# Float32 decoder trunk on one core: weight halves made by GpSimd transfers (cast, then accumulate) in place of a raw buffer and a subtraction

## The chip, the cores and the metric

The kernel runs on one core of one Trainium2 chip. The metric is the device time of one execution in microseconds (us). Below, PE is the matrix engine, ACT the scalar engine, DVE the vector engine, POOL the GpSimd engine and SP the engine that mostly issues transfers. Each of SP, ACT and POOL can issue transfers in its own queue, and each engine works through its instructions strictly in the order in which they stand.

## The reference, cut to what matters

Two layers over 512 tokens of width 1024, everything in float32:

```
for l in range(DEPTH):
    h = rmsnorm(x, g_mix[l])
    dq, dk, dv, c_q, c_kv_kr, xq, gate_logits = split(h @ w_in[l])
    y_diff = diff_attention(dq, dk, dv, ...) @ w_diff_o[l]        # 8 heads, causal
    y_mla  = latent_attention(c_q, c_kv_kr, ...) @ w_mla_o[l]     # 8 heads, causal
    y_mem  = memory_cross_attention(xq, mem_n, ...) @ w_cross_o[l]
    gates  = sigmoid(gate_logits + b_gate[l])
    merged = gates[0] * y_diff + gates[1] * y_mla + gates[2] * y_mem
    x = x + merged @ w_out[l]
    x = x + square(relu(rmsnorm(x, g_mlp[l]) @ w_mlp1[l])) @ w_mlp2[l]
```

## The kernel before

**Three multiplications for one.** PE multiplies in a reduced float format (`fp32r` in the profile). To keep float32 accuracy each operand is split into a high part `hi`, which is the value rounded to that format, and a low part `lo = value - hi`. The helper `mm3` (L108 to L111) then issues three matmuls into the same sum: hi·hi (L109), one cross term (L110) and the other (L111).

**Weight units.** All weights are cut on the host into units of at most 128 x 1024 numbers (512 KB), 320 in all, listed in `units` in the order of use. A unit goes through three stages. `load_raw` (L901) has SP transfer it into one of `RB` = 3 raw buffers `wraw`. `do_split` (L908) calls `split_into` (L100): ACT copies `wraw` into `whi` with rounding (L101), and DVE writes `wlo = wraw - whi` (L102). Then PE reads both. There are `NB` = 4 buffers each of `whi` and `wlo`, so splits run up to four units ahead of use and raw loads three further. The other activations are split by the same helpers: `split_scaled` (L104) makes ACT write hi (L105) and DVE lo (L106), both with a gain per row.

**Order of the work.** `prog` is a list of entries, one for each piece of a stage, with the units that it reads. `merge` interleaves attention entries with matrix products by a fixed plan, so that PE has products to do while ACT and DVE work on softmaxes. In each layer come the projections (`ck_item`, `cq_item`, `kvb_item`, `qb_item`, `diff_chunk`, gates), attention, the output projections (`y8_item`, `out_item`), and last the MLP: 32 `u_item` and 32 `w2_item`, one unit and 24 matmuls of 512 columns each. A scheduler turns the program order into one fixed order for each engine; it works with estimates of time, and the order is then fixed for the chip.

**The start.** `begin` (L293) has SP load the eight tiles of x, with the first three raw loads between them (`if k in (0, 2, 5): load_raw()`), and `feed` splits each x tile on ACT and DVE. The first product is `ck_item`, with three units.

**POOL** builds constants at the start and computes the power -1/2 in `rsq` (L131, L132) for the norms, 91 instructions of 128 x 2 to 128 x 8 numbers. Their results `f`, `of`, `r` are read by DVE (L587, L666 and others), and PE then transposes what DVE wrote (L591, L669). It issues no transfer.

Of the kernel before, what the change touches and what calls it, by code (L numbers as in the profile page):

```python
# [9 lines left out]
F32 = mybir.dt.float32  # L10
F32R = mybir.dt.float32r
AF = mybir.ActivationFunctionType
ALU = mybir.AluOpType
AX = mybir.AxisListType

P = 128
# [43 lines left out]
def tile_trunk(ctx: ExitStack, tc: tile.TileContext, x_t, mem_t, mem_n, pos, ifr, gcol, grow, w_ck, w_cq, w_kvb, w_qb,  # L60
               w_mem, w_xq, w_d, w_g, w_oc, w_om, w_od, w_out, w_1, w_2, out):
    nc = tc.nc
    V, A, G, T = nc.vector, nc.scalar, nc.gpsimd, nc.tensor

    def pool(name, bufs, **kw):
        return ctx.enter_context(tc.tile_pool(name=name, bufs=bufs, **kw))

    RB, NB = 3, 4
    cst = pool("cst", 1)
    sm = pool("sm", 2)  # L70
    pw_raw, pw_hi, pw_lo = pool("wraw", RB), pool("whi", NB), pool("wlo", NB)
    pools = {n: pool(n, b) for n, b in (("H", 16), ("O", 16), ("X", 8), ("G", 1), ("B", 24), ("scr", 5), ("PT", 4))}
    p_p = pool("P", 3)
    PS = {n: pool("ps_" + n, b, space=bass.MemoryType.PSUM) for n, b in (("acc", 2), ("s", 3), ("tp", 2), ("o", 1))}
    dram = pool("dram", 1, space=bass.MemoryType.DRAM)
# [2 lines left out]
    def nm(s):  # L78
        cnt[0] += 1
        return f"{s}{cnt[0]}"  # L80

    def tl(which, dt=F32):
        return pools[which].tile([P, 512], dt, tag=which, name=nm(which))
# [16 lines left out]
    def split_into(hi, lo, src):  # L100
        A.activation(out=hi, in_=src, func=AF.Copy)  # L101
        V.tensor_tensor(out=lo, in0=src, in1=hi, op=ALU.subtract)  # L102
# [116 lines left out]
    def feed(l, k, xt, gbase, dst, sqs):  # L219
        hi, lo = tl(dst, F32R), tl(dst, F32R)  # L220
        split_scaled(hi, lo, xt, gc[:, l, gbase + k:gbase + k + 1])
        if k == 0:
            A.activation(out=sqs, in_=xt, func=AF.Square)
        else:
            s = tl("scr")
            A.activation(out=s, in_=xt, func=AF.Square)
            V.tensor_tensor(out=sqs, in0=sqs, in1=s, op=ALU.add)
        return hi, lo

    def new_sqs():  # L230
        return tl("scr")
# [47 lines left out]
    def layer(l):  # L279
# [13 lines left out]
        def begin():  # L293
            if l == 0:
                sqs = new_sqs()
                h = []
                xts = []
                for k in range(KT):
                    xt = tl("X")
                    nc.sync.dma_start(out=xt, in_=x_t[k * P:(k + 1) * P, :])  # L300
                    xts.append(xt)
                    if k in (0, 2, 5):
                        load_raw()
                for k, xt in enumerate(xts):
                    h.append(feed(0, k, xt, C_MIX, "H", sqs))
                st["h"], st["sqs"] = h, sqs
            s["h"] = st["h"]
# [550 lines left out]
        def dpair(p):  # L858
            return diff_chunk(p, 0) + diff_chunk(p, 1) + diff_chunk(p, 2)

        e = [Entry(lambda w: begin())]
        gx = [gate_item(1, ft, "X") for ft in range(KT)]
        ym = [y4_item(w_om, "om", 1, fp, True) for fp in range(4)]
# [31 lines left out]
        prog.extend(layer(l))  # L895

    units = [ap for e in prog for ap in e.units]
    raws, splits = [], []
    consumed = 0

    def load_raw():  # L901
        ap = units[len(raws)]
        a, b = ap.shape[1], ap.shape[2]
        t = pw_raw.tile([P, 1024], F32, tag="wraw", name=nm("wraw"))
        nc.sync.dma_start(out=t[:, :a * b].rearrange("p (a b) -> p a b", a=a), in_=ap)
        raws.append((t, a, b))

    def do_split():  # L908
        t, a, b = raws[len(splits)]
        hi = pw_hi.tile([P, 1024], F32R, tag="whi", name=nm("whi"))  # L910
        lo = pw_lo.tile([P, 1024], F32R, tag="wlo", name=nm("wlo"))
        split_into(hi[:, :a * b], lo[:, :a * b], t[:, :a * b])
        splits.append(tuple(z[:, :a * b].rearrange("p (a b) -> p a b", a=a) for z in (hi, lo)))

    for i, e in enumerate(prog):
        if i == 0:
            e.fn([])
            continue
        while len(splits) < min(len(units), consumed + NB):
            while len(raws) < min(len(units), len(splits) + RB):  # L920
                load_raw()
            do_split()
        while len(raws) < min(len(units), len(splits) + RB):
            load_raw()
        n = len(e.units)
        e.fn(splits[consumed:consumed + n])
        consumed += n

# [80 lines left out]
```

## Time and profile before

| | |
|---|---|
| median of 3 runs | 2035.04 us (2034.2 to 2037.99) |
| the profiled execution | 2039.67 us, its span 2037.6 us, mean granted PE clock 0.994 |
| PE busy | 2005.1 us, 98% |
| weight loads of PE (beside the matmuls) | 1715.9 us, 84% |
| DVE busy | 1162.2 us, 57% |
| ACT busy | 917.4 us, 45% |
| POOL busy | 146.0 us, 7%, 121 instructions |
| transfers | 181 MB, mean 89 GB/s |

The span runs from the first to the last instruction; the execution's own time holds a little more around it. Busy times are those of the engine's own instructions. A matmul's end is modelled, so successive matmuls overlap in the records. In the groups of instructions a row reads: line, engine, operation, output <- inputs, shapes, count, busy us, mean ns of one, then the idle time just before and what ended most of it.

### The profile page before, as it was taken

The page shows a single profiled execution, that of the slowest core. Times are in us where ns is not written, and L with a number is a line of the kernel's source. Part 1 is how long each engine was busy: PE and PEld are TensorE (multiplying, and loading weights), DVE is VectorE, ACT ScalarE, POOL GpSimd, SP SyncE. Part 2 cuts the span into 40 slices and gives each one's busy share as a digit, 9 for nine tenths or more (in the row PEclk, how much of TensorE's full clock was granted, in tenths as well). Part 3 has the DMA queues.
Part 4 walks back from the last instruction along what each step waited for, and adds up shares of the span by engine and source line. Part 5 has one row for each costly group of instructions (what it writes and reads, how often), then busy time and mean ns, then how long its engine had stood idle before and what let it go on. Part 6 is the DMA issues. An engine that isn't in the chain of part 4 may idle for free.

```text
span 2037.6 us, 27922 instructions
## 1 busy us (share of the span) xinstructions
PE 2005.1 (98%) x11008; PEld 1715.9 (84%) x11008; DVE 1162.2 (57%) x2170; ACT 917.4 (45%) x1727; POOL 146.0 (7%) x121
## 2 busy tenths in 40 slices
PE   8999999999999999999999999999999999999999
PEld 7779997888878888888888899979897788888887
DVE  7755765777656543434447567757686454434442
ACT  6666654444433432323346666634445334323321
POOL 0300110111200000000002001101020000000000
PEclk9989999999999999999999999999999999999999
DMA  5233122222214333333332321222222333333332
GB/s 170 73 110 102 69 63 73 63 73 73 63 53 154 93 96 101 93 99 98 117 104 67 125 80 63 72 74 63 73 63 63 101 116 93 102 96 94 102 94 73
DMA packets 54675, 181.06 MB, mean 89 GB/s; under 512 B 6416, under 2 KB 7440, under 8 KB 54544
## 3 DMA queue, kind: packets, MB, share of 16 engines
q1 hardware_dynamic: 51840, 175.66, 27.8%
q10 hardware_dynamic: 2704, 3.62, 0.6%
q8 instruction: 87, 1.43, 0.3%
q14 instruction: 44, 0.36, 0.1%
HBM read 175.06 MB, written 4.19 MB: 88 GB/s over the span
## 4 chain that ended last, share of the span: by engine, by line
PE 95%; ACT 2%; DVE 1%; DMA 1%; issue 0%; POOL 0%; ACTq 0%; DVEq 0%; POOLq 0%
PE psacc L109 21%; PE psacc L111 20%; PE psacc L110 20%; PE pss L109 7%; PE pss L111 7%; PE pss L110 7%; PE pss L610 2%; PE pss L613 2%; PE pso L642 2%; PE pstp L654 1%; PE pstp L638 1%; PE pstp L591 1%; PE pso L110 1%; PE pso L111 1%; PE pso L109 1%; PE pstp L479 1%
## 5 line engine op out<-in xcount | busy, mean ns | idle before, releaser
L101 ACT ACTIVATE whi<-wraw 128x1024 fp32r<-128x1024 f32 (+3 forms) x320 | 334.5, 1046 | 751.7 <-PE psacc L110 398.5
L102 DVE TENSOR_TENSOR wlo<-wraw,whi 128x1024 fp32r<-128x1024 f32 (+3 forms) x320 | 385.9, 1206 | 97.7 <-ACT whi L101 95.4
L109 PE MATMUL psacc<-H,whi 128*128 128x512 f32 x816 | 321.6, 394 | 2.6 <-ACT B L561 2.2
L110 PE MATMUL psacc<-H,whi 128*128 128x512 f32 x816 | 320.2, 392 | 0.0
L111 PE MATMUL psacc<-H,wlo 128*128 128x512 f32 x816 | 320.1, 392 | 0.0
L109 PE MATMUL psacc<-whi,H 128*128 128x256 f32 (+1 forms) x928 | 271.6, 294 | 10.3 <-ACT whi L101 6.8
L110 PE MATMUL psacc<-wlo,H 128*128 128x256 f32 (+1 forms) x928 | 265.1, 286 | 0.0
L111 PE MATMUL psacc<-whi,H 128*128 128x256 f32 (+1 forms) x928 | 264.3, 287 | 0.2 <-DVE H L106 0.2
L109 PE MATMUL pss<-O,whi 128*128 128x512 f32 x640 | 249.8, 392 | 1.6 <-ACT O L105 1.6
L110 PE MATMUL pss<-O,whi 128*128 128x512 f32 x640 | 250.8, 392 | 0.0
L111 PE MATMUL pss<-O,wlo 128*128 128x512 f32 x640 | 250.5, 392 | 0.0
L109 PEld LDWEIGHTS psacc<-whi,H 128*128 128x128 f32 x928 | 177.6, 192 | 17.8 <-ACT whi L101 6.8
L109 PEld LDWEIGHTS psacc<-H,whi 128*128 128x128 f32 x816 | 153.2, 188 | 36.0 <-ACT B L561 2.6
L111 PEld LDWEIGHTS psacc<-H,wlo 128*128 128x128 f32 x816 | 153.2, 188 | 33.6 <-issue 2.0
L110 PEld LDWEIGHTS psacc<-H,whi 128*128 128x128 f32 x816 | 153.3, 188 | 31.4 <-issue 0.7
L110 PEld LDWEIGHTS psacc<-wlo,H 128*128 128x128 f32 x928 | 178.2, 192 | 1.8 <-issue 1.0
L111 PEld LDWEIGHTS psacc<-whi,H 128*128 128x128 f32 x928 | 177.3, 192 | 1.0 <-DVE H L106 0.4
L840 DVE TENSOR_TENSOR X<-psacc,X 128x512 f32<-128x512 f32 x64 | 44.3, 692 | 207.1 <-PE psacc L111 207.1
L627 ACT ACTIVATE P<-pss,nmx 128x128 f32<-128x128 f32 (+2 forms) x224 | 115.1, 521 | 73.6 <-DVE nmx L624 47.5
L109 PEld LDWEIGHTS pss<-O,whi 128*128 128x128 f32 x640 | 120.4, 188 | 27.3 <-ACT O L105 2.0
L110 PEld LDWEIGHTS pss<-O,whi 128*128 128x128 f32 x640 | 121.1, 189 | 25.5 <-DVE O L106 0.3
L111 PEld LDWEIGHTS pss<-O,wlo 128*128 128x128 f32 x640 | 121.0, 189 | 24.9
(231 smaller groups left out, 3220.6 us busy)
## 6 DMA issues: line engine op xcount, KB each, us to landing
wraw<-in_w_dram SPq DMA_DIRECT2D x128, 512.0 KB, 3.6
wraw<-in_w_g_dram SPq DMA_DIRECT2D x48, 512.0 KB, 3.6
wraw<-in_w_d_dram SPq DMA_DIRECT2D x48, 512.0 KB, 3.6
wraw<-in_w_mem_dram SPq DMA_DIRECT2D x16, 512.0 KB, 3.7
wraw<-in_w_od_dram SPq DMA_DIRECT2D x16, 512.0 KB, 3.6
wraw<-in_w_out_dram SPq DMA_DIRECT2D x16, 512.0 KB, 3.7
X<-in_x_t_dram SPq DMA_DIRECT2D x16, 256.0 KB, 5.4
wraw<-in_w_xq_dram SPq DMA_DIRECT2D x8, 512.0 KB, 4.3
```

What stands on the lines that cost most here:

```text
L101: A.activation(out=hi, in_=src, func=AF.Copy)
L102: V.tensor_tensor(out=lo, in0=src, in1=hi, op=ALU.subtract)
L109: T.matmul(o, lhsT=l[0], rhs=r[0], start=first, stop=False, **kw)
L110: T.matmul(o, lhsT=l[0], rhs=r[1], start=False, stop=False, **kw)
L111: T.matmul(o, lhsT=l[1], rhs=r[0], start=False, stop=last, **kw)
L479: T.transpose(tp_[:96, t * P:(t + 1) * P], in_=src[t][:, h * 96:(h + 1) * 96], identity=ident)
L591: T.transpose(tp_[:, h * 256 + t * P:h * 256 + (t + 1) * P], in_=y[:, t * 256 + h * P:t * 256 + (h + 1) * P], identity=ident)
L610: T.matmul(sw[m][:, :max(N, 256)], lhsT=qk[m][0][a], rhs=qk[m][1][b], start=i == 0, stop=i == 2)
L613: T.matmul(sv[m], lhsT=qk[m][0], rhs=qk[m][1], start=True, stop=True)
L627: A.activation(out=pt[:, m, :N], in_=sv[m], func=AF.Exp, bias=nmx[:, m:m + 1], accum_out=ssum[m])
L642: T.matmul(o, lhsT=w[:, j * P:(j + 1) * P], rhs=vs(j), start=j == 0, stop=j == nb - 1)
L840: V.tensor_tensor(out=xt, in0=q, in1=xt, op=ALU.add)
```

## The change

The raw buffers and SP's weight loads go away. For each unit `do_split` now has POOL issue a transfer straight from the float32 weight into `whi`, which rounds on the way because the target's type is `fp32r`. ACT writes the negative of it into `wlo` (`Copy` with scale -1, L908 in the new file). A second POOL transfer of the same weight adds it into `wlo` (`accum_op=ALU.add`, L901 in the new file), which leaves weight - hi. This second transfer is issued by `low()`, one unit late: after the next unit's first transfer and its ACT instruction, or earlier when the next entry needs it. DVE's subtraction for the weights (L102 on `wlo`) is gone. `NB` grows from 4 to 5, the pool `B` shrinks from 24 tiles to 23, the descriptor area for POOL's transfers grows from 2048 to 8192 bytes for each partition, and `begin` no longer places weight loads between the x tiles.

```diff
-    RB, NB = 3, 4
+    NB = 5
-    pw_raw, pw_hi, pw_lo = pool("wraw", RB), pool("whi", NB), pool("wlo", NB)
+    pw_hi, pw_lo = pool("whi", NB), pool("wlo", NB)
-    pools = {... ("B", 24) ...}
+    pools = {... ("B", 23) ...}
...
-                    if k in (0, 2, 5):
-                        load_raw()
...
-    def load_raw():
-        ap = units[len(raws)]
-        ...
-        nc.sync.dma_start(out=t[:, :a * b].rearrange("p (a b) -> p a b", a=a), in_=ap)
-        raws.append((t, a, b))
+    def low():
+        lo, hi, ap = todo.pop(0)
+        G.dma_start(out=lo, in_=ap, accum_op=ALU.add)
 
     def do_split():
-        t, a, b = raws[len(splits)]
-        ...
-        split_into(hi[:, :a * b], lo[:, :a * b], t[:, :a * b])
+        ap = units[len(splits)]
+        ...
+        G.dma_start(out=hi, in_=ap)
+        A.activation(out=lo, in_=hi, func=AF.Copy, scale=-1.0)
+        todo.append((lo, hi, ap))
+        splits.append((hi, lo))
+        while len(todo) > 1:
+            low()
...
         n = len(e.units)
+        while len(splits) - len(todo) < consumed + n:
+            low()
         e.fn(splits[consumed:consumed + n])
...
-    nc = _bacc.Bacc("TRN2", ..., dynamic_dma_scratch_size=2048)
+    nc = _bacc.Bacc("TRN2", ..., dynamic_dma_scratch_size=8192)
```

**Place one, the start, first transfers.** SP's queue before, from its first row: x tiles (`X`) with weight loads (`wraw`) between them.

```order
L300 DMA X_140<-in_x_t_dram 128x512
L905 DMA wraw_142<-in_w_ck_dram 128x576
L300 DMA X_144<-in_x_t_dram 128x512
L300 DMA X_146<-in_x_t_dram 128x512
L905 DMA wraw_148<-in_w_ck_dram 128x864
L300 DMA X_150<-in_x_t_dram 128x512
L300 DMA X_152<-in_x_t_dram 128x512
L300 DMA X_154<-in_x_t_dram 128x512
L905 DMA wraw_156<-in_w_ck_dram 128x864
```

Now SP issues the eight x tiles and nothing else there, and the weights stand in POOL's queue, behind its constants (`mask` is the last of them):

```order
masks.py:30 AFFINE_SELECT mask<-mask 128x128
L907 DMA whi_207<-in_w_ck_dram 128x576
L907 DMA whi_211<-in_w_ck_dram 128x864
L907 DMA whi_216<-in_w_ck_dram 128x864
L907 DMA whi_221<-in_w_cq_dram 128x1024
L907 DMA whi_226<-in_w_cq_dram 128x1024
L901 DMA wlo_208<-in_w_ck_dram 128x576
L901 DMA wlo_212<-in_w_ck_dram 128x864
L901 DMA wlo_217<-in_w_ck_dram 128x864
```

All five first `whi` transfers now stand ahead of the first accumulating one, though the program asks for that one after the second.

**Place two, the start, PE.** PE's first products of `ck_item` after the change; those before stand in the same order, with L109, L110 and L111 on `whi_216`, `wlo_217` and `H_162`.

```order
L109 MATMUL psacc_231<-whi_207,H_153 128x288
L109 MATMUL psacc_232<-whi_207,H_153 128x288
L109 MATMUL pss_233<-whi_207,H_153 128x288
L109 MATMUL pss_234<-whi_207,H_153 128x288
L110 MATMUL psacc_231<-wlo_208,H_153 128x288
```

Only four products stand ahead of the first that reads a low part, as before the change.

**Place three, POOL in the attention of layer 0**, where the cross queries are normed and the weights `w_d` of the differential projections are fetched. Before, POOL has only the powers `f` here:

```order
L132 TENSOR_TENSOR f_2129<-e_2127,mhalf 128x4
L132 TENSOR_TENSOR f_2171<-e_2169,mhalf 128x4
L132 TENSOR_TENSOR f_2337<-e_2335,mhalf 128x4
L132 TENSOR_TENSOR f_2379<-e_2377,mhalf 128x4
L132 TENSOR_TENSOR f_2569<-e_2567,mhalf 128x8
```

Now the same powers stand between transfers:

```order
L907 DMA whi_2052<-in_w_d_dram 128x1024
L132 TENSOR_TENSOR f_2091<-e_2089,mhalf 128x4
L901 DMA wlo_2053<-in_w_d_dram 128x1024
L907 DMA whi_2143<-in_w_d_dram 128x1024
L132 TENSOR_TENSOR f_2133<-e_2131,mhalf 128x4
L907 DMA whi_2241<-in_w_d_dram 128x1024
L901 DMA wlo_2144<-in_w_d_dram 128x1024
L901 DMA wlo_2242<-in_w_d_dram 128x1024
L132 TENSOR_TENSOR f_2297<-e_2295,mhalf 128x4
L907 DMA whi_2349<-in_w_d_dram 128x1024
L132 TENSOR_TENSOR f_2339<-e_2337,mhalf 128x4
```

Each `whi` row waits for PE to leave a buffer, each `wlo` row for ACT's negative, and a power behind them waits with them.

More of the change, by code (lines that the diff above doesn't have):

```diff
@@ L66, in pool @@
         return ctx.enter_context(tc.tile_pool(name=name, bufs=bufs, **kw))
-    RB, NB = 3, 4
+    NB = 5
     cst = pool("cst", 1)
     sm = pool("sm", 2)
-    pw_raw, pw_hi, pw_lo = pool("wraw", RB), pool("whi", NB), pool("wlo", NB)
-    pools = {n: pool(n, b) for n, b in (("H", 16), ("O", 16), ("X", 8), ("G", 1), ("B", 24), ("scr", 5), ("PT", 4))}
+    pw_hi, pw_lo = pool("whi", NB), pool("wlo", NB)
+    pools = {n: pool(n, b) for n, b in (("H", 16), ("O", 16), ("X", 8), ("G", 1), ("B", 23), ("scr", 5), ("PT", 4))}
     p_p = pool("P", 3)
@@ L897, in tile_trunk, with do_split @@
     units = [ap for e in prog for ap in e.units]
-    raws, splits = [], []
+    splits, todo = [], []
     consumed = 0
-    def load_raw():
-        ap = units[len(raws)]
-        a, b = ap.shape[1], ap.shape[2]
-        t = pw_raw.tile([P, 1024], F32, tag="wraw", name=nm("wraw"))
-        nc.sync.dma_start(out=t[:, :a * b].rearrange("p (a b) -> p a b", a=a), in_=ap)
-        raws.append((t, a, b))
-    def do_split():
-        t, a, b = raws[len(splits)]
-        hi = pw_hi.tile([P, 1024], F32R, tag="whi", name=nm("whi"))
-        lo = pw_lo.tile([P, 1024], F32R, tag="wlo", name=nm("wlo"))
-        split_into(hi[:, :a * b], lo[:, :a * b], t[:, :a * b])
-        splits.append(tuple(z[:, :a * b].rearrange("p (a b) -> p a b", a=a) for z in (hi, lo)))
+    def low():
+        lo, hi, ap = todo.pop(0)
+        G.dma_start(out=lo, in_=ap, accum_op=ALU.add)
+    def do_split():
+        ap = units[len(splits)]
+        a, b = ap.shape[1], ap.shape[2]
+        hi, lo = (pw.tile([P, 1024], F32R, tag=t, name=nm(t))[:, :a * b].rearrange("p (a b) -> p a b", a=a) for pw, t in ((pw_hi, "whi"), (pw_lo, "wlo")))
+        G.dma_start(out=hi, in_=ap)
[4 more added lines that the diff above has]
+            low()
     for i, e in enumerate(prog):
@@ L919, in tile_trunk @@
         while len(splits) < min(len(units), consumed + NB):
-            while len(raws) < min(len(units), len(splits) + RB):
-                load_raw()
             do_split()
-        while len(raws) < min(len(units), len(splits) + RB):
-            load_raw()
         n = len(e.units)
+        while len(splits) - len(todo) < consumed + n:
+            low()
         e.fn(splits[consumed:consumed + n])
@@ L996 @@
     data = _layout(_np, {k: _np.asarray(v) for k, v in inputs.items()})
-    nc = _bacc.Bacc("TRN2", target_bir_lowering=False, num_devices=1, dynamic_dma_scratch_size=2048)
+    nc = _bacc.Bacc("TRN2", target_bir_lowering=False, num_devices=1, dynamic_dma_scratch_size=8192)
     arrays, args = {}, []
```

## Prediction

> **What bounds the kernel now.** I read the page first: busy times, the chain that ended last, the groups.
>
> ```profile
> PE 2005.1 (98%) x11008; PEld 1715.9 (84%) x11008; DVE 1162.2 (57%) x2170; ACT 917.4 (45%) x1727; POOL 146.0 (7%) x121
> PE 95%; ACT 2%; DVE 1%; DMA 1%; issue 0%; POOL 0%; ACTq 0%; DVEq 0%; POOLq 0%
> L101 ACT ACTIVATE whi<-wraw 128x1024 fp32r<-128x1024 f32 (+3 forms) x320 | 334.5, 1046 | 751.7 <-PE psacc L110 398.5
> L102 DVE TENSOR_TENSOR wlo<-wraw,whi 128x1024 fp32r<-128x1024 f32 (+3 forms) x320 | 385.9, 1206 | 97.7 <-ACT whi L101 95.4
> ```
>
> PE is the chain. The 385.9 us of DVE that the change removes lie beside it, and so do ACT's 334.5 us, most of whose wait ahead is for PE to leave a buffer. The chip can win at most what PE idles: 2037.6 - 2005.1 = 32.5 us. Who PE waited for, from the list of waits (total us, times, longest):
>
> ```profile
> PE psacc L109 <- ACT whi L101: 6.8, 1, 6.8
> PE psacc L109 <- DVE B L106: 5.7, 4, 1.7
> PE psacc L109 <- ACT O L105: 3.5, 2, 2.6
> PE pstp L669 <- DVE scr L666: 2.1, 2, 1.1
> PE psacc L111 <- DVE H L106: 0.2, 1, 0.2
> ```
>
> 6.8 us are the start. Waits for DVE are 5.7 + 2.1 + 0.2 = 8.0 us: that is all a lighter DVE can give directly.
>
> **Term 1, taken off DVE and SP.** 320 subtractions go, -386 us of DVE, and SP's 320 issues. Neither is on the path. Of the 8.0 us I take 3, since a DVE that starts sooner still waits for the ACT high part ahead of it (L105 before L106). Bounds 0 and 8.
>
> **Term 2, ACT.** Still 320 instructions of 128x1024, SBUF to SBUF, by the L101 row 1046 ns each: no change of busy time. Its wait changes: before, for PE to leave `whi`; now for that and then a whole transfer. Queued behind it are softmax exponentials and copies out of PSUM.
>
> **Term 3, the steady supply.** The tightest stage is the MLP: one unit per ACT row there.
>
> ```profile
> 803.48 1.06 ACT L101 ACTIVATE whi<-wraw 128x1024 fp32r<-128x1024 f32 x1 [4.38 <-PE psacc L110]
> 808.92 1.06 ACT L101 ACTIVATE whi<-wraw 128x1024 fp32r<-128x1024 f32 x1 [4.38 <-PE psacc L110]
> 700.00:1000.00 300.00, 300.00 (x1325) 248.42 (x1324) 126.88 (x144) 94.85 (x118) 0.00 (x0) 1.00 0.32 98
> 150.00:550.00 400.00, 395.69 (x2689) 352.66 (x2688) 273.81 (x593) 211.66 (x468) 50.74 (x36) 1.00 0.23 72
> 12.00:14.00 2.00, 2.00 (x17) 2.00 (x17) 1.90 (x4) 2.00 (x4) 0.00 (x0) 1.00 1.07 413
> wraw<-in_w_dram SPq DMA_DIRECT2D x128, 512.0 KB, 3.6
> ```
>
> A unit every 808.92 - 803.48 = 5.44 us. In the windows the last two columns are the transfer engines' share and GB/s: 0.32 x 5.44 = 1.74 us of all 16 engines for one plain unit when they are idle, and 512 KB at 413 GB/s = 1.27 us when they are full. So the first transfer costs 1.27 to 1.74 if rounding costs nothing. No row shows an accumulating transfer. Its lower bound is one plain transfer, 1.27. Its upper bound is three separate passes (read the weight, read `wlo`, write), 3 x 1.74 = 5.2. The pair thus needs 2.5 to 7.0 us against 5.44. I take two passes, since reads and writes run beside each other in a plain copy already: 1.74 + 3.48 = 5.2 with idle engines, 3 x 1.27 = 3.8 with full ones. It fits, barely, and costs nothing. In attention a unit comes every 512 KB / 72 GB/s = 7.3 us, which holds even 7.0.
>
> The Trainium skill, "Collectives: The Full Stack", The bandwidth ceiling, says that an adding transfer is half as fast as a copy because it reads two sources, the add itself being free. By that the pair would cost the 5.2 or 3.8 that I took; no row here shows it.
>
> Latency is covered. The buffer of unit i is free when PE ends unit i-5, so 4 x 5.44 = 21.8 us remain. The chain is transfer 3.6 (row above), ACT 1.06, one unit that `low` lags, 5.44, and the accumulating transfer, at most 3.6 + 2 x 1.74 = 7.1: 17.2 us.
>
> POOL's cost to issue a transfer is not shown either; I bound it by SP's issue and by POOL's dearest group.
>
> ```profile
> L905 SPq DMA_DIRECT2D wraw<-in_w_dram x128: 327/328/333, 646.2 to 1998.0; - x128
> L132 POOL TENSOR_TENSOR f<-e,mhalf 128x8 f32<-128x8 f32 x32 | 66.6, 2080 | 183.9 <-DVE e L573 109.3 <-DVE e L575 74.6
> ```
>
> 0.33 to 2.08 us, so 640 issues are 211 to 1331 us, and two per unit 0.7 to 4.2 of 5.44: not a bound. I take 1 us, between the two and nearer SP's row, which is the same work.
>
> **Term 4, the start.** Rows of the timeline (start us, us) and windows:
>
> ```profile
> 1.45 0.29 POOL masks.py:30 TENSOR_SCALAR_AFFINE_SELECT mask<-mask 128x128 f32<-128x128 f32 x1
> 7.91 0.45 PE L110 MATMUL psacc<-wlo,H 128*128 128x288 f32 x1
> 20.37 0.74 DVE H L106
> 24.94 0.71 ACT L409 ACTIVATE O<-psacc 128x288 f32<-128x288 f32 x2
> 2.00:4.00 2.00, 0.00 (x0) 0.00 (x0) 0.25 (x4) 0.38 (x1) 0.00 (x0) 1.00 1.01 317
> ```
>
> Now PE's first low product is at 7.91, the last low part of x is ready at 20.37 + 0.74 = 21.1 (from the chain), and `ck_item` ends at 24.9. After the change eight x tiles of 256 KB (2.1 MB) and five `whi` (288 + 432 + 432 + 512 + 512 KB, 2.2 MB) are asked for at once, from 1.7 us on, with the first accumulating transfer behind all five on POOL. At 390 GB/s, between the windows with 317 and 413, 4.3 MB take 11 us, until 13; two passes of 288 KB take 1.5; and 3.6 - 1.74 = 1.9 is the fixed part of a landing, of which about 1 is not covered: the first `wlo` lands near 15.5 to 16, 8 us late. `ck_item` has 96 products, 15 us from there with the slow first ones (7.91 to 24.9 now, less the 2 us that PE waits for x): it ends near 31 in place of 24.9. I take +6. The low end: if the first `wlo` passes the later `whi` it lands at 10.5, when x is still the limit: 0. The high end: issues of 2.08 us put the fifth `whi` at 1.7 + 5 x 2.08 = 12.1 and the first `wlo` at 12.1 + 2.1 + 7.1 = 21: +13 on the first product, less the 2 us of waits, +11.
>
> The Trainium skill, "DMA: Bandwidth & Descriptors", Queues, rings and completion order, says that a queue's pieces are taken in order on each engine and queues take turns. By that the first `wlo` comes last and the +6 stands; otherwise 0.
>
> **Term 5, POOL's powers behind transfers.** The norm chain of one projection:
>
> ```profile
> 221.55 0.16 DVE L573 TENSOR_TENSOR e<-ss,ex 128x8 f32<-128x8 f32 x1
> 221.85 1.69 POOL L132 TENSOR_TENSOR f<-e,mhalf 128x8 f32<-128x8 f32 x1 [10.07 <-DVE e L573]
> 224.57 0.69 DVE L587 TENSOR_TENSOR scr<-scr,f 128x512 f32<-128x512 f32 x1
> 228.12 0.49 PE L591 MATMUL pstp<-ident,scr 128*128 128x128 f32 x3
> L132 POOL TENSOR_TENSOR of<-e,mhalf 128x4 f32<-128x4 f32 x16 | 16.8, 1050 | 504.9 <-DVE e L755 456.5 <-DVE c L630 48.4
> ```
>
> DVE's result is ready at 225.26, PE takes it at 228.12: 2.9 us of slack. A power behind one issue (1 us) is hidden. Behind a `wlo` issue it also waits for landing and negative, up to 3.6 + 1.06 = 4.7, which passes the slack by 1.8. The new order puts most powers right behind a `whi` and ahead of the `wlo`, a few behind a `wlo` (f_2297). There are 68 `f` and 16 `of`; if one in ten is caught at half of that excess, 8 x 0.9 = 7, and half of those waits are taken up by products that stand in between: +4. Bounds 0 and 84 x 1.8 = 151.
>
> **Sum**, against the profiled execution of 2039.67 (span 2037.6 and 2 us around it): -3 + 0 + 0 + 6 + 4 = +7, so 2047. That execution lies 4.6 above the median of 2035.04; on the median's level I forecast 2042, own range 2034 to 2056. For this kernel 0.2% (4.1 us) is about what a measurement can tell from no change.
>
> **Rivals.**
>
> *The transfers become the bound.* Place: the MLP and the projections just before it, 600 to 1040 and 1600 to 2013 us, 853 us or 157 units at 5.44. It decides from 5.44 us per pair on. At 6.2 us, midway to the bound of 7.0, 157 x 0.76 = +119, 2161 with the forecast's other terms; at 7.0, +245, 2287. For it: nothing measured says that rounding is free, and 5.2 is close to 5.44. Against: full engines move a unit in 1.27, not 1.74. Issues of over 2.72 us on POOL would look the same.
>
> *POOL's order hurts.* If a quarter of the 84 powers is caught by the full 1.8 us: +38 in place of +4, 2076. For it: PE's order is fixed with 2.9 us of slack, and ACT also stands still behind a late negative. Against: ACT now waits 4.38 us at L101 without holding up PE.
>
> *Faster.* The first `wlo` is served before the later `whi` (start 0), DVE's 8.0 us of waits go entirely, no power is caught: 2035 - 8 = 2027. It decides at the start: it needs `wlo_208` landed by 10.5. For it: a third of DVE's work goes, and DVE holds up POOL:
>
> ```profile
> 512.93 5.63 POOL L132 TENSOR_TENSOR f<-e,mhalf 128x8 f32<-128x8 f32 x1 [0.36 <-DVE e L575]
> ```
>
> This power took 5.63 us, not 1.69, while DVE worked without a gap, the removed L102 among its work. Against: PE barely waited there.
>
> **How the numbers follow.** Forecast 0.42, of which 0.26 above 2039, 0.13 within 0.2%, 0.03 below 2031. Transfers bound 0.20. POOL's order 0.18. Faster 0.20. So slower 0.26 + 0.20 + 0.18 = 0.64, same 0.13, faster 0.23. The range for 8 in 10, 2024 to 2220, leaves out the worse part of the transfer case (0.08) and a gain of over 11 us (0.05).
>
> **What the profile after would show.** Right: DVE near 776 us, ACT near 917; the MLP still at 5.44 us per unit with the transfer share under 0.96; PE's first low product near 15.5; few waits of PE on L132's readers. Wrong: a transfer share near 1 in the MLP and PE waiting for `wlo`; PE waiting at L591 or L669 in many places; or a first low product before 11. The forecast falls if an accumulating transfer takes more than 5.44 - 1.74 = 3.7 us of the engines, or a POOL issue over 2.72.

## The result, and the profile after

The changed kernel takes 2359.94 us (2354.83 to 2368.45, four runs) against 2034.88 us (2034.20 to 2037.99): 1.159 times as long, 95% interval [1.156, 1.163]. The forecast was 2042 and its range ended at 2220. The profiled execution has a span of 2366.7 us, 329.1 more than before. The lines of the page that answer to those shown of before (engine row, shares of the chain, ACT's group at the weights, landing of the transfers):

```profile
PE 2120.5 (90%) x11008; PEld 1775.3 (75%) x11008; DVE 797.1 (34%) x1850; ACT 912.2 (39%) x1727; POOL 602.4 (25%) x761
issue 56%; POOL 16%; PE 11%; DMA 10%; DVE 3%; ACT 3%; POOLq 0%; ACTq 0%
L908 ACT ACTIVATE wlo<-whi 128x1024 fp32r<-128x1024 f32 (+3 forms) x320 | 334.2, 1045 | 1179.0 <-DMA whi<-in_w_dram 589.7
whi<-in_w_dram POOLq DMA_DIRECT2D x128, 512.0 KB, 6.9
wlo<-in_w_dram POOLq DMA_DIRECT2D x128, 512.0 KB, 5.7
```

DVE is relieved as meant, ACT does as much as before, and no engine is full. But the chain is no longer PE: it runs through POOL's issues, the transfers that they start, and "issue", time for which the chain's own record names no cause. The list of waits (total us, times, longest) names it:

```profile
POOL wlo L901 <- ACT wlo L908: 1258.5, 260, 9.3
ACT wlo L908 <- DMA whi<-in_w_dram: 589.7, 102, 9.7
PE psacc L111 <- DMA wlo<-in_w_dram: 34.4, 17, 4.6
PE psacc L109 <- DVE X L838: 24.5, 10, 6.1
PE pss L608 <- ACT P L625: 23.9, 11, 5.0
```

PE's own waits are many small ones with different names: those of over 0.15 us add up to 112.3 us for ACT, 67.8 for low parts and 48.6 for DVE (20.3, 0 and 8.0 before). The big number is POOL's: more than half of the span it stands at an accumulating transfer, which waits for ACT's negative, which waits for the cast to land. Here is that in the MLP, in the timeline of POOL and ACT (start us, us, instruction, idle time before it and its releaser):

```profile
954.38 0.85 POOL L901 DMA_DIRECT2D wlo<-in_w_dram  x1 [8.00 <-ACT wlo L908]
954.93 1.41 POOL L907 DMA_DIRECT2D whi<-in_w_dram  x2
961.15 1.06 ACT L908 ACTIVATE wlo<-whi 128x1024 fp32r<-128x1024 f32 x1 [5.88 <-DMA whi<-in_w_dram]
962.51 0.87 POOL L901 DMA_DIRECT2D wlo<-in_w_dram  x1 [6.17 <-ACT wlo L908]
963.30 1.04 ACT L908 ACTIVATE wlo<-whi 128x1024 fp32r<-128x1024 f32 x1
964.64 0.88 POOL L901 DMA_DIRECT2D wlo<-in_w_dram  x1 [1.26 <-ACT wlo L908]
965.19 0.89 POOL L907 DMA_DIRECT2D whi<-in_w_dram  x1
973.32 0.85 POOL L901 DMA_DIRECT2D wlo<-in_w_dram  x1 [7.25 <-ACT wlo L908]
973.87 1.42 POOL L907 DMA_DIRECT2D whi<-in_w_dram  x2
```

Read it downwards. The casts at 954.93, 965.19 and 973.87 have no idle time before them: their buffers are free when POOL comes to them. Going by PE's last product on each buffer, the first and the third had been free for some 8 us, the second for 1.3. They are late because they stand on POOL behind an accumulating transfer that waits for the cast before them. So it is a loop: cast, landing, negative, accumulating transfer, and only then the next cast. From 954.93 to 973.87 it makes three units in 18.94 us, 6.3 a unit, where PE takes 5.44. In POOL's order 225 of the 320 accumulating transfers stand with no later cast ahead of them, and 87 with one, although the program writes every one but the last behind the cast of the next unit.

Windows of the same place show what the transfer engines do meanwhile (window, us, busy time of PE, PEld, DVE, ACT and POOL, granted clock, transfer share, GB/s):

```profile
800.00:1150.00 350.00, 314.55 (x1320) 252.09 (x1319) 54.66 (x83) 89.47 (x111) 75.47 (x106) 0.97 0.70 164
959.00:961.00 2.00, 2.00 (x10) 1.44 (x10) 0.00 (x0) 0.00 (x0) 0.00 (x0) 1.00 1.11 395
966.00:970.00 4.00, 2.25 (x10) 1.88 (x11) 1.29 (x2) 0.04 (x1) 0.07 (x1) 1.00 1.05 198
972.00:974.00 2.00, 2.00 (x10) 1.65 (x9) 0.00 (x0) 1.97 (x3) 0.68 (x2) 1.00 0.00 0
```

Casts run at 395 GB/s, accumulating transfers at 198, and between them the engines stand still. Over the MLP their share is 0.70: they are not the bound.

The 329.1 us of span are 213.7 us more of idle PE (2366.7 - 2120.5 = 246.2, before 32.5) and 115.4 us more of busy PE. A good part of the latter is PE's clock, which was halved more often:

```profile
core 0: 2366.7 us, clock 0.950
core 0: 2037.6 us, clock 0.994
```

The clock is 1 or 0.5, so (1 - 0.950) x 2 x 2366.7 = 237 us ran at half speed, before 24. By the trace's clock records PE was busy for 196 of these 237 us (before for 23), and half the difference, some 87 us, is what the half clock added to its busy time by this estimate. Where the other 28 of the 115.4 us come from is not shown.

### The profile page after: what moved, and what is told of

Its sections match the earlier page's. It is cut to its first block, busy times and chain, and to the rows that moved or that the text cites. A ratio compares the mean times of both kernels' runs of the same rounds, so it can differ in the third digit from the quotient of the medians.

```text
span 2366.7 us, 28092 instructions
## 1 busy us (share of the span) xinstructions
PE 2120.5 (90%) x11008; PEld 1775.3 (75%) x11008; DVE 797.1 (34%) x1850; ACT 912.2 (39%) x1727; POOL 602.4 (25%) x761
## 4 chain that ended last, share of the span: by engine, by line
issue 56%; POOL 16%; PE 11%; DMA 10%; DVE 3%; ACT 3%; POOLq 0%; ACTq 0%
POOL whi L907 7%; POOL wlo L901 7%; DMA whi<-in_w_d_dram 4%; DMA whi<-in_w_g_dram 3%; PE psacc L109 3%; PE psacc L111 3%; PE psacc L110 2%; POOL f L132 2%; ACT wlo L908 1%; PE pss L608 1%; PE pss L611 1%; DVE ss L566 1%; PE pso L640 1%; DMA whi<-in_w_dram 1%; DMA whi<-in_w_om_dram 0%
## 5 line engine op out<-in xcount | busy, mean ns | idle before, releaser
L908 ACT ACTIVATE wlo<-whi 128x1024 fp32r<-128x1024 f32 (+3 forms) x320 | 334.2, 1045 | 1179.0 <-DMA whi<-in_w_dram 589.7
L109 PE MATMUL psacc<-H,whi 128*128 128x512 f32 x816 | 335.4, 411 | 29.6 <-ACT O L407 11.1
L111 PE MATMUL psacc<-H,wlo 128*128 128x512 f32 x816 | 332.4, 408 | 18.2 <-DMA wlo<-in_w_dram 18.2
L110 PE MATMUL psacc<-H,whi 128*128 128x512 f32 x816 | 329.8, 405 | 0.0
L109 PE MATMUL psacc<-whi,H 128*128 128x256 f32 (+1 forms) x928 | 276.7, 299 | 16.2 <-DMA whi<-in_w_ck_dram 9.5
L111 PE MATMUL pss<-O,wlo 128*128 128x512 f32 x640 | 256.6, 402 | 23.8 <-DMA wlo<-in_w_dram 22.7
L110 PE MATMUL psacc<-wlo,H 128*128 128x256 f32 (+1 forms) x928 | 269.6, 291 | 7.8 <-DMA wlo<-in_w_ck_dram 7.8
L901 POOL DMA_DIRECT2D wlo<-in_w_dram x128 | 111.2, 868 | 636.0 <-ACT wlo L908 611.4
L111 PE MATMUL psacc<-whi,H 128*128 128x256 f32 (+1 forms) x928 | 269.2, 290 | 0.0
L109 PE MATMUL pss<-O,whi 128*128 128x512 f32 x640 | 253.9, 398 | 11.2 <-ACT O L105 11.2
L110 PE MATMUL pss<-O,whi 128*128 128x512 f32 x640 | 253.7, 397 | 0.0
L109 PEld LDWEIGHTS psacc<-H,whi 128*128 128x128 f32 x816 | 160.8, 197 | 69.7 <-ACT O L407 11.2
L111 PEld LDWEIGHTS psacc<-H,wlo 128*128 128x128 f32 x816 | 160.0, 196 | 59.1 <-DMA wlo<-in_w_dram 23.8
L109 PEld LDWEIGHTS psacc<-whi,H 128*128 128x128 f32 x928 | 181.2, 196 | 25.1 <-issue 14.1
L110 PEld LDWEIGHTS psacc<-wlo,H 128*128 128x128 f32 x928 | 181.4, 196 | 10.7 <-DMA wlo<-in_w_ck_dram 8.4
L110 PEld LDWEIGHTS psacc<-H,whi 128*128 128x128 f32 x816 | 160.3, 196 | 32.8
L111 PEld LDWEIGHTS psacc<-whi,H 128*128 128x128 f32 x928 | 181.2, 195 | 0.3
L111 PEld LDWEIGHTS pss<-O,wlo 128*128 128x128 f32 x640 | 123.3, 193 | 56.6 <-DMA wlo<-in_w_dram 30.0
L109 PEld LDWEIGHTS pss<-O,whi 128*128 128x128 f32 x640 | 123.0, 192 | 38.3 <-ACT O L105 12.6
L110 PEld LDWEIGHTS pss<-O,whi 128*128 128x128 f32 x640 | 123.1, 192 | 26.7 <-DVE O L106 0.5
L838 DVE TENSOR_TENSOR X<-psacc,X 128x512 f32<-128x512 f32 x64 | 43.7, 689 | 253.3 <-PE psacc L111 253.3
```

What stands on the lines that cost most here:

```text
L109: T.matmul(o, lhsT=l[0], rhs=r[0], start=first, stop=False, **kw)
L110: T.matmul(o, lhsT=l[0], rhs=r[1], start=False, stop=False, **kw)
L111: T.matmul(o, lhsT=l[1], rhs=r[0], start=False, stop=last, **kw)
L838: V.tensor_tensor(out=xt, in0=q, in1=xt, op=ALU.add)
L901: G.dma_start(out=lo, in_=ap, accum_op=ALU.add)
L908: A.activation(out=lo, in_=hi, func=AF.Copy, scale=-1.0)
```

## The experiments

The table gives each kernel's median and ratio to the kernel before (runs of that chip), and the profiled span cut at two rows of DVE in each layer: the first result of the MLP (L824 in the changed kernel) and its last (L838). So the four parts are all up to the first MLP, the MLP, attention and projections of the second layer, and its MLP. Each kernel but the one before ran four times, e9_none_ahead twice. The code below shows the main lines of each edit alone.

| kernel | us | ratio, 95% interval | to MLP | MLP 0 | attention 1 | MLP 1 |
|---|---|---|---|---|---|---|
| before | 2034.9 | 1 | 694.5 | 332.9 | 674.3 | 332.9 |
| changed | 2359.9 | 1.159 [1.156, 1.163] | 787.7 | 401.8 | 779.9 | 393.1 |
| e1_lag1 | 2105.2 | 1.034 [1.031, 1.037] | 726.2 | 334.5 | 701.1 | 332.9 |
| e2_lag2 | 2116.9 | 1.039 [1.037, 1.041] | 738.9 | 332.9 | 705.2 | 334.5 |
| e9_none_ahead | 2765.0 | 1.358 [1.355, 1.361] | 870.2 | 519.1 | 852.7 | 516.3 |
| e4_no_hi | 2051.8 | 1.007 [1.005, 1.008] | 706.2 | 333.3 | 673.3 | 333.3 |
| e3_plain_low | 2075.8 | 1.018 [1.016, 1.020] | 712.7 | 334.4 | 690.4 | 334.4 |
| e7_cast_alone | 2062.9 | 1.014 [1.012, 1.015] | 704.8 | 334.2 | 682.6 | 334.2 |
| e8_accumulate_alone | 2068.4 | 1.016 [1.015, 1.018] | 710.1 | 334.4 | 683.4 | 334.4 |
| e5_negative_on_dve | 2106.3 | 1.035 [1.034, 1.037] | 730.1 | 332.9 | 703.5 | 333.0 |
| e11_act_stands | 2078.7 | 1.020 [1.018, 1.022] | 716.7 | 332.9 | 690.8 | 332.9 |
| e6_first_pair | 2103.8 | 1.033 [1.030, 1.036] | 730.4 | 334.5 | 699.6 | 332.9 |
| e10_late_negative | 2255.7 | 1.108 [1.106, 1.111] | 790.1 | 345.5 | 769.8 | 345.8 |
| e12_later_negative | 2132.9 | 1.047 [1.045, 1.050] | 735.9 | 339.0 | 712.3 | 339.6 |

### POOL's order: one cast ahead, two, none

```
# e1_lag1: keep the written order on POOL (e2_lag2: while len(todo) > 2)
-        G.dma_start(out=lo, in_=ap, accum_op=ALU.add)
+        with tc.issue_after(last[-1]):          # last: the casts, in order
+            G.dma_start(out=lo, in_=ap, accum_op=ALU.add)
...
-        G.dma_start(out=hi, in_=ap)
+        last.append(G.dma_start(out=hi, in_=ap).ins)
```

> Edit: each accumulating transfer is queued on POOL behind the casting transfer of the unit after it, as the source writes it (in the changed kernel 225 of the 320 accumulating transfers are queued right behind their own unit's casting transfer, with no later one ahead). All transfers and instructions stay. Theory 1, POOL's in-order queue makes a serial loop (cast 6.9 us landing, negative 1.05, issues 0.55 and 0.87, then only the next unit's cast): with one cast ahead the loop of 9.4 us serves two units, 4.7 us a unit, under the 5.44 that PE needs, so the MLP goes back to about 335 us a layer (402 and 393 now) and the time to 2050-2120. Theory 2, the pair of transfers takes too much of the transfer engines: order does not matter, the MLP stays at 6.3-6.7 us a unit and the time at 2310-2400. Theory 3, POOL's powers and ACT's negatives that stand behind transfers hurt in attention: there are none of the powers in the MLP, so the MLP alone recovers (-125) and attention does not: 2220-2260.

> Edit: as with one cast ahead, but each accumulating transfer is queued on POOL behind the casting transfers of the two units after it. Theory 1: the loop of 9.4 us now serves three units, 3.1 us a unit, and POOL's wait at the accumulating transfer (1258.5 us in all now) falls under 100 us; MLP 333 us a layer, time 2040-2090, no slower than with one cast ahead. Theory 2: 2310-2400, MLP 6.3-6.7 us a unit. Theory 3: 2220-2260, with attention as slow as now.

One cast ahead takes 254.8 us off, 78% of the loss, with the same transfers and instructions, and the MLP is back at 333 to 335 us. POOL's timeline there:

```profile
907.74 0.55 POOL L908 DMA_DIRECT2D whi<-in_w_dram  x1 [2.78 <-PE psacc L111]
908.30 0.88 POOL L902 DMA_DIRECT2D wlo<-in_w_dram  x1
913.18 0.55 POOL L908 DMA_DIRECT2D whi<-in_w_dram  x1 [4.00 <-PE psacc L111]
914.61 0.85 POOL L902 DMA_DIRECT2D wlo<-in_w_dram  x1 [0.88 <-ACT wlo L909]
```

A cast every 913.18 - 907.74 = 5.44 us, and what it waits for is PE again, to leave a buffer. Theory 2 (the transfers' own time) falls with this run. With two casts ahead POOL's wait at the accumulating transfer falls from 215.9 us to 20.7, but the time is 11.7 us longer and lies above the 2040 to 2090 expected: POOL's wait was no longer what cost. Each accumulating transfer now stands later, which fits PE's waits for low parts (15.0 us in all with one cast ahead, 26.2 with two). The opposite edit puts every cast behind the accumulating transfer of the unit before:

```
# e9_none_ahead (from the second unit on)
+            with tc.issue_after(last[-1]):      # last: the accumulating transfers
                 G.dma_start(out=hi, in_=ap)
...
-        while len(todo) > 1:
+        while todo:
```

> Edit: each cast is queued on POOL behind the accumulating transfer of the unit before it, so that none of the 320 has a later cast ahead of it (225 had none in the changed kernel). The same transfers and instructions. Theory 1: the loop is now paid by every unit: the changed kernel's MLP shows three units and two loops in 19.5 us, 9.75 a loop, so 9.0-9.8 us a unit; 333 us of MLP become 550-600 a layer, attention's 7.0 us a unit become 8.5-9.5, and the time 2800-3050. Theory 2, the transfers' own time: order costs nothing, 2310-2400.

```profile
1008.50 0.88 POOL L909 DMA_DIRECT2D whi<-in_w_dram  x1
1016.53 0.87 POOL L901 DMA_DIRECT2D wlo<-in_w_dram  x1 [7.16 <-ACT wlo L912]
1017.08 0.89 POOL L909 DMA_DIRECT2D whi<-in_w_dram  x1
880.00:1380.00 500.00, 388.29 (x1432) 296.85 (x1431) 68.40 (x99) 107.16 (x130) 85.68 (x120) 0.90 0.56 128
```

Every unit now pays the loop, 1017.08 - 1008.50 = 8.6 us here and 8.4 on average over the window, and the transfer share falls to 0.56. The time lies 35 us under what I expected: the 9.75 us that I took (19.5 / 2) was a mean over the changed kernel's loops with two casts (in the stretch above 965.19 - 954.93 = 10.3) and with one (973.87 - 965.19 = 8.7), and here all have one. From none ahead over the changed order to one ahead the MLP goes 518, 397, 334 us.

### The members of the loop

```
# e4_no_hi: the accumulating transfer no longer depends on the cast
-        A.activation(out=lo, in_=hi, func=AF.Copy, scale=-1.0)
+        A.activation(out=lo, in_=<a constant, broadcast>, func=AF.Copy, scale=0.0)
# e3_plain_low: overwrite in place of adding
-        G.dma_start(out=lo, in_=ap, accum_op=ALU.add)
+        G.dma_start(out=lo, in_=ap)
```

> Edit: ACT's instruction reads a constant in place of the high part and writes zeros, with the same size (left out: the negative, so the low part is the whole weight). The accumulating transfer then no longer waits for the cast's landing; all transfers stay, 308 of 320 accumulating ones right behind their own unit's cast. Theory 1: POOL's wait of 1258.5 us at the accumulating transfer falls to under 300, the MLP is back at 333-340 us a layer, time 2040-2110. Theory 2: the same bytes and passes, 2310-2400. Theory 3: MLP recovers, attention keeps the powers behind transfers: 2150-2260.

Without the dependence all but 14 us is gone (the kernel before took 2037.4 in these runs), though all 640 transfers run, and the second layer's attention takes 673.3 us, 1.0 less than before the change. The window over the MLP:

```profile
710.00:1035.00 325.00, 325.00 (x1436) 269.10 (x1435) 70.23 (x102) 104.67 (x134) 84.09 (x119) 1.00 0.94 196
```

PE has no gap, and the transfer engines are at 0.94: 0.94 x 5.44 = 5.1 us for a pair. So the pair fits, with 6% to spare. The 11.7 us that remain lie ahead of the first MLP, and most of them in the start, below: in the first 50 us PE is busy for 32.85 us, before for 42.34. The smaller pool `B` is in this kernel too, and its attention pays nothing for it.

> Edit: the second transfer of each unit overwrites instead of adding (left out: the adding, so the low part is the whole weight). Order of all queues as in the changed kernel. Theory 1: the loop stays, and only what the next cast waits for the second transfer in the rings falls, at most 2.6 - 1.3 = 1.3 us of a loop of 9.4 that runs for most units: 2230-2345, POOL's wait at the second transfer still over 900 us. Theory 2: the second pass of the adding transfer is gone, 3.5 us of engines a pair at most, the MLP is back at 5.44 us a unit: 2040-2120.

The time lies 154 us below the range. POOL's order is that of the changed kernel, row for row, and the wait at the second transfer is still 962 us, as expected; but the MLP is back at 334 us.

```profile
905.02 0.53 POOL L907 DMA_DIRECT2D whi<-in_w_dram  x1 [3.18 <-PE psacc L111]
908.09 0.53 POOL L901 DMA_DIRECT2D wlo<-in_w_dram  x1 [2.53 <-ACT wlo L908]
910.98 0.54 POOL L907 DMA_DIRECT2D whi<-in_w_dram  x1
917.35 0.53 POOL L901 DMA_DIRECT2D wlo<-in_w_dram  x1 [5.83 <-ACT wlo L908]
917.88 0.54 POOL L907 DMA_DIRECT2D whi<-in_w_dram  x1
```

The loop with one cast is 917.88 - 910.98 = 6.9 us, where it was 8.7: the cast lands in 4.6 us in place of 6.9, and the transfer issued ahead of it in 3.9 in place of 5.7. That brings three units under 3 x 5.44 us, and the cast at 905.02 waits for PE again. My range came from an error: even the 1.3 us a loop that I allowed make 2 x 1.3 of 19.5 us, 5.6 us a unit, and 277 us over two loops for every three of 320 units: 2083, not 2230. So this run does not tell the two theories apart, since both now give about what it shows; e1_lag1, e9_none_ahead and e4_no_hi do, with every adding transfer in place. Read with them, what the adding costs in the changed kernel is most likely the length that it gives the loop, by standing in front of the next cast.

### Each half alone

```
# e7_cast_alone, from the kernel before: ACT's cast becomes a transfer
-        split_into(hi, lo, t)
+        G.dma_start(out=hi, in_=ap);  V.tensor_tensor(out=lo, in0=t, in1=hi, op=ALU.subtract)
# e8_accumulate_alone, from the kernel before: ACT's cast stays
-        split_into(hi, lo, t)
+        A.activation(out=hi, in_=t, func=AF.Copy);  A.activation(out=lo, in_=hi, func=AF.Copy, scale=-1.0)
+        G.dma_start(out=lo, in_=ap, accum_op=ALU.add)
```

> Edit, from the kernel before: the high part by a casting transfer on POOL; SP's raw load and DVE's subtraction stay as they were, ACT's 320 casts go (B has 23 buffers, as in the changed kernel). No transfer waits for a landing, so there is no loop. Theory 1: MLP 333 us a layer; ACT loses 334 us of work, PE idles 32.5 us at most to be won; the first high part lands later than ACT's (9 us in place of 6.8): 2025-2045. Rival: the cast itself, at 5.2-6.9 us of landing against 3.6, is too slow for PE: 2070 or more, with PE waiting for whi.

> Edit, from the kernel before: SP's raw load and ACT's cast stay, ACT also writes the negative from the high part, and the accumulating transfer on POOL adds the weight, with no subtraction on DVE (B has 23 buffers). The accumulating transfers are all there, 320 of them, but nothing on POOL stands before the raw load, which is on SP. Theory 1: no loop, MLP 333-338 us a layer; ACT has 334 us more (1250, 61%), which may cost PE up to 20 a layer in attention: 2035-2080. Theory 2, the adding is dear in itself: 2200 or more with the MLP over 380 a layer.

Neither half has the loop, since in neither does a cast or a raw load stand behind an accumulating transfer in one queue. And neither wins: +28 and +33 us. The second one shows what POOL's wait is worth by itself:

```profile
POOL wlo L914 <- ACT wlo L913: 1290.4, 274, 12.4
```

POOL stands at the accumulating transfer for longer than in the changed kernel (1258.5 us), and the MLP is at 334 us. So the size of that wait is no measure of the loss; what counts is what stands behind it. The cast alone missed its range at the upper side: it took the 320 casts off ACT (busy for 609.8 us in place of 917.4), and DVE now stands for casts in ACT's place (538 us of waits ahead of the subtraction). PE's waits for DVE rise from 8.0 to 25.1 us. A relieved engine that is not the bound gave nothing; that the new wait on an engine that serves the softmax is what cost fits these rows, but no run takes it away alone.

### What is left with one cast ahead

It is 60.1 us of profiled parts over the kernel before: 31.7 up to the first MLP, 26.8 in the second attention, 1.6 in the MLPs. Does it come from the engine that stands until a cast has landed?

```
# e5_negative_on_dve (on e1_lag1)
-        A.activation(out=lo, in_=hi, func=AF.Copy, scale=-1.0)
+        V.tensor_scalar(out=lo, in0=hi, scalar1=-1.0, scalar2=None, op0=ALU.mult)
# e11_act_stands (on e4_no_hi): ACT waits for the cast, the unit's second transfer does not
+        A.activation(out=<128 x 1 scratch>, in_=hi[:, 0, 0:1], func=AF.Copy)
```

> Edit: as with one cast ahead (2105.2), and DVE writes the negative in place of ACT. What is left there over the kernel before is 12 at the start and 27 a layer in attention. Theory A, ACT standing behind negatives that wait for a cast's landing (some 620 us of such waits in all, with softmax exponentials queued behind) makes the 27 a layer: attention recovers to within 5 a layer, 2045-2070; ACT near 585 us busy. Theory B, POOL's powers behind the accumulating transfers make it: no change, 2095-2120. Theory C, DVE queues its own work behind the negative and passes the delay on as ACT did: 2085-2130, with PE waiting for DVE in place of ACT.

> Edit: as with the constant in place of the high part (2051.8; the low part is again the whole weight), and after its write ACT reads one column of the high part, a tiny instruction of some 0.1-0.2 us whose result nobody uses. ACT then stands until the cast has landed, as it does with one cast ahead, but the unit's accumulating transfer does not wait for that. Theory C, the engine that stands for a landing passes the delay to the softmax and copies behind it, and this is the 27 a layer that is left with one cast ahead: attention 690-705 us in the second layer against 673, time 2075-2110. Theory B, POOL's order and powers are what is left: attention stays at 675, time 2050-2062.

DVE in ACT's place changed nothing in the time (attention 703.5 against 701.1). But PE's waits moved along: 35.2 us for DVE and 13.5 for ACT, where one cast ahead has 12.5 and 35.2. That is the sign of theory C, and against theory B, for which only the time would fit. It does not say how much of the 60 us the standing costs; the next run does for a part. In the list of groups of e11_act_stands:

```profile
L909 ACT ACTIVATE tiny<-whi 128x1 f32<-128x1 f32 x320 | 65.0, 203 | 739.4 <-DMA whi<-in_w_dram 415.8 <-DMA whi<-in_w_d_dram 73.3 <-DMA whi<-in_w_g_dram 68.3
```

320 instructions of 0.2 us, before each of which ACT stands for a cast, cost 26.9 us (2078.7 - 2051.8): 10.5 up to the first MLP and 17.5 in the second attention, nothing in the MLPs. The 65 us of ACT's work are hardly the price: ACT is busy for 46%, and e8_accumulate_alone, which gives it 334 us more, has an attention 9.1 us longer. POOL's order is that of e4_no_hi, but its wait for ACT rose from 195 to 285 us, since the next unit's write on ACT stands behind the tiny one, so a part may be POOL's. Against a large one: PE's waits for low parts did not rise (8.5 us, now 8.0), those for ACT did (16.1, now 29.0). This is some 27 of the 53 us between e4_no_hi and e1_lag1. The other half was not separated: there POOL's order differs, and the accumulating transfer itself waits for its unit's landing.

If standing costs, ACT should do the negative later, when the cast has landed:

```
# e10_late_negative (three units ahead), e12_later_negative (four)
 def low():
+    neg = A.activation(out=lo, in_=hi, func=AF.Copy, scale=-1.0)   # no longer in do_split
+    if consumed > 3:
+        tc.keep_in_program_order(neg)           # behind ACT's work traced so far
... (the accumulating transfer behind the newest cast, as in e1_lag1)
-    while len(splits) - len(todo) < consumed + n:
+    while len(splits) - len(todo) < min(len(units), consumed + max(n, 3)):   # or 4
```

> Edit: ACT's negative of a unit is queued on ACT three units ahead of its use (it stood about five ahead, where the cast has just been issued), behind ACT's work of the units before, and the accumulating transfer behind it; casts still run five ahead. ACT then finds the cast landed. Theory C, whichever engine writes the negative stands until the cast has landed and passes that on to the softmax and copies queued behind it: ACT's waits for whi (620 us in all with one cast ahead) fall under 150 and attention recovers, 2045-2075 (the start's 12 stays). Theory B, POOL's powers queue behind accumulating transfers and casts that wait for a buffer: no change, 2095-2120. Third way, the accumulating transfer is now too late for PE (16 us ahead against 1.05 + 0.87 + 7.4 = 9.3): PE waits for wlo, over 2120.

> Edit: as with the late negative (2255.7), but queued on ACT four units ahead of its use in place of three, so that the accumulating transfer has one unit (5.44 us) more. Theory: the late negative lost because the second transfer came too late for PE; with one unit more the low part is in time in the MLP (333-336 us against 345) and ACT seldom stands for a landing: 2060-2100. Rival: the negatives bunch behind ACT's own work in program order and POOL waits for them in attention: 2120-2200.

Both lost, in the ranges of the third way and of the rival. ACT's waits for `in_w` casts fell (372.3 us with one cast ahead, 166.1 and 195.3 now), but PE waits for low parts that come late: 113.4 and 54.8 us in all, where one cast ahead has 15.0. The longest of them, first e10_late_negative, then e12_later_negative:

```profile
PE psacc L110 <- DMA wlo<-in_w_qb_dram: 21.0, 4, 5.4
PE psacc L110 <- DMA wlo<-in_w_d_dram: 18.5, 10, 4.3
```

```profile
PE psacc L111 <- DMA wlo<-in_w_g_dram: 19.9, 6, 4.2
PE pss L111 <- DMA wlo<-in_w_od_dram: 8.7, 2, 4.4
```

POOL waits for the negative for over 517 us in both. In these runs five buffers hold too little lead to serve both: a negative early makes ACT stand, a negative late makes PE stand. No run has more buffers.

### The start

Rows of the changed kernel's timeline:

```profile
9.51 0.82 PE L109 MATMUL psacc<-whi,H 128*128 128x288 f32 x2 [9.51 <-DMA whi<-in_w_ck_dram]
10.38 0.87 POOL L901 DMA_DIRECT2D wlo<-in_w_ck_dram  x1 [5.83 <-ACT wlo L908]
18.62 0.61 PE L110 MATMUL psacc<-wlo,H 128*128 128x288 f32 x1 [7.81 <-DMA wlo<-in_w_ck_dram]
32.63 0.81 ACT L407 ACTIVATE O<-psacc 128x288 f32<-128x288 f32 x2 [2.43 <-PE psacc L111]
```

PE waits for the first cast until 9.5 us, and the first accumulating transfer takes 8.2 us from its issue to the product that waits for it, among x tiles and other casts. That it is issued only when the first cast has landed is not the reason. In e4_no_hi it is issued at 7.62 us, and the product starts no earlier than 18.45:

```profile
7.62 2.68 POOL L901 DMA_DIRECT2D wlo<-in_w_ck_dram  x3 [3.05 <-ACT wlo L908]
18.45 0.61 PE L110 MATMUL psacc<-wlo,H 128*128 128x288 f32 x1 [7.97 <-DMA wlo<-in_w_ck_dram]
```

It waits for what was asked for ahead of it. Windows of the changed kernel, with GB/s last:

```profile
2.00:4.00 2.00, 0.00 (x0) 0.00 (x0) 0.09 (x2) 0.21 (x1) 2.00 (x5) 1.00 0.99 294
4.00:10.00 6.00, 0.49 (x2) 0.52 (x3) 1.91 (x7) 3.43 (x6) 0.56 (x2) 1.00 0.91 280
10.00:18.00 8.00, 0.81 (x4) 0.46 (x2) 5.74 (x9) 7.34 (x13) 2.59 (x3) 1.00 1.12 342
```

The next run gives the first accumulating transfer the right of way:

```
# e6_first_pair (on e1_lag1): the first unit's pair, then the casts of units two to five
+        if len(splits) == 1:
+            low()                                # and hi of unit two behind it
```

> Edit: as with one cast ahead (2105.2), and on POOL the first unit's accumulating transfer stands right behind its cast, ahead of the casts of units two to five. Theory start: the first low product waits 8.1 us behind five casts; with the pair first it comes near 11-12 in place of 17-18, the wait falls to about 2, and the time by 5-8: 2095-2101. Rival: the x tiles and the casts share the engines anyway and x is the limit: within 3 of 2105.

```profile
14.56 0.61 PE L110 MATMUL psacc<-wlo,H 128*128 128x288 f32 x1 [3.82 <-DMA wlo<-in_w_ck_dram]
23.38 0.61 PE L110 MATMUL psacc<-wlo,H 128*128 128x288 f32 x1 [2.93 <-DMA wlo<-in_w_ck_dram]
35.87 0.69 ACT L407 ACTIVATE O<-psacc 128x288 f32<-128x288 f32 x2
```

The first low product comes 3.9 us earlier than the 18.41 of e1_lag1, and `ck_item` ends no earlier (35.87 against 34.83): PE now waits at 23.38 for the second unit's low part, which comes later. The time, 2103.8 in place of 2105.2, is within the spread of the runs and above the 2095 to 2101 of the theory; it is what the rival gave, but not for the rival's reason, since what PE waits for is a weight and not x. No run found a version faster than the kernel before.

## Why the prediction was wrong, point by point

**Term 1, DVE and SP (-3).** DVE is at 797 us, 21 above the 776 that were forecast. The gain can be seen only where nothing hides it: in e4_no_hi PE's waits for DVE are 2.2 us in place of 8.0, some 6 us less, within the bounds of 0 and 8 and twice the 3 that were taken. In the changed kernel they are longer than before, 48.6 us.

**Term 2, ACT (0).** The busy time is right: 334.2 us for 1045 ns each. The wait was named, with softmax and copies behind it, and priced at nothing. It costs: up to 27 us in e11_act_stands, of which a part may be POOL's.

**Term 3, the steady supply. This is the step that failed.** Its first half held to a tenth: 5.2 us for a pair was forecast, e4_no_hi shows 5.1, and accumulating at 198 GB/s against 395 is the two passes that I took. The Trainium skill, "Collectives: The Full Stack", The bandwidth ceiling, says of the reduce step of collectives that it is half as fast as a copy because the add reads two sources, and the trace agrees in the ratio. POOL's issues, 0.55 and 0.87 us, were under the 1 us taken. What failed is "Latency is covered". I summed the chain of one unit, 17.2 us, against the 21.8 us for which its buffer is free. With the measured numbers that sum still holds: 6.9 + 1.06 + 5.44 + 5.7 = 19.1, though 225 units do not even have the lag of one unit in it. But it assumes that a cast starts when its buffer is free. On POOL's one in-order queue it starts when the accumulating transfer ahead of it has been let go, and that one waits for the landing of an earlier cast. I used exactly this for the powers in term 5 ("behind a `wlo` issue it also waits for landing and negative") and not for the casts, whose rows stand behind `wlo` rows in the order shown. Price: the MLPs, 68.9 + 60.2 us, and most of the 199 us before and between them; e1_lag1 gives back 254.8.

**Term 4, the start (+6).** 11.7 us up to the first MLP in e4_no_hi, just over the bounds of 0 and 11. The first low product came at 18.6, not 15.5 to 16, and `ck_item` ended at 32.6, not 31. The order was read rightly, the first accumulating transfer comes last. The mis-sized step is the rate: 390 GB/s were taken for the transfers ahead of it, and the windows show 280 to 342.

**Term 5, POOL's powers (+4).** In e4_no_hi all powers stand behind transfers and attention 1 takes 1.0 us less than before. Where the transfers don't wait for landings, the powers cost nothing that shows; in the changed kernel itself I did not separate them.

**What no term held:** the half clock. PE idles for 213.7 us more and is busy for 115.4 us more, of which some 87 are the half clock by the estimate above.

**The rivals.** "The transfers become the bound" lies nearest in time (2161 to 2287) but is the wrong mechanism: its sign was a share near 1 with PE waiting for `wlo`, and the share was 0.70; with the share at 0.94 the kernel is fast. "POOL's order hurts" had the right queue and the wrong victim. "Faster" needed the first low part landed by 10.5 us, and its transfer was issued only at 10.38. DVE and ACT came out near the list of signs; 5.44 us per unit and the low product at 15.5 did not.

## What to carry to other kernels

Two transfers of which the second needs the first one's landing should not share an in-order queue without others in between: count, in the order as built, how many first transfers stand ahead of each second one, and compare the loop (issue, landing, the work between, issue), divided by the units in it, with the time that the consumer takes per unit. The total of the queue's waits does not tell, since e8_accumulate_alone has as much of it without the loop. A lead in buffers is worth nothing if the queue does not use it. And work moved off an engine that isn't the bound bought nothing here, while an engine that is made to stand for a landing delays all that is queued behind it.

## What the hardware showed that was not expected

Half-clock intervals of PE often follow gaps of some 2 us. Over the fourteen profiled executions, of PE's gaps after the first 60 us, these had a half-clock interval (3.4 us or a multiple) at their end or within 3.5 us after it: 14 of 229 gaps of 0.3 to 1 us, 69 of 211 of 1 to 2 us, 118 of 166 of 2 to 3 us, 100 of 101 of over 3 us. The Trainium skill, "TensorE: Matmul & The Clock Gate", HAM oscillation — how this bites in real kernels, gives the rule that no gap should be over about 3.4 us; here gaps well below that went with the half clock too. That the gaps cause it is read from the order in time; no run set gaps alone.

The other surprise was how steep such a loop is: 1.8 us less in a loop of 8.7 (e3_plain_low) took 284 us off. By the pattern of the MLP, two loops for three units, it is paid some 213 times, until the loop passes under PE's pace.
